# Up-projection weight sums formed by accumulating transfers instead of VectorE subtractions

## The chip, the cores and the metric

The kernel runs on one core of a Trainium2 chip. The metric is the device time of one execution in microseconds (us), the median of several runs. A core has a matrix engine (TensorE, PE in the profile; PEld is its weight load), VectorE (DVE), ScalarE (ACT), GpSimd (POOL) and SyncE (SP). Each engine works through its own queue in order. Transfers between DRAM and the on-chip memory (SBUF) are issued from the queues of SP, ACT or POOL and run on 16 transfer engines. Matrix products are summed in PSUM banks.

## What is computed

One decoder layer: two token mixers, a projection with a residual, a squared-ReLU MLP with a residual, and a gated embedding at the end. All inputs are float32. The change touches the first product of the MLP alone (cut from the reference; 512 tokens, `w_up` is 1024 x 4096, `w_down` 4096 x 1024):

```python
v = rms_norm(h, norm_pre_mlp[i])
ff = jnp.square(jax.nn.relu(v @ w_up[i])) @ w_down[i]
h = h + rms_norm(ff, norm_post_mlp[i])
```

## The kernel before

For precision every float32 operand is split into two parts, hi and lo (`split`, L59 to L61: ACT casts hi, DVE subtracts to get lo), and a product is three matmuls: hi by hi, hi by lo, lo by hi. A weight block is loaded into a `raw` tile of 128x1024 (512 KB), and `pair_of` splits it into a `whi`/`wlo` pair. There are six raw buffers and six pairs in this stage, two pools each, taken in turns.

The MLP works in four quarters. A quarter is two groups of the up product (`up_group`, L1020) and one down product (`down`, L1082), which runs 24 matmuls into each of eight accumulation sets (two column halves c by four token tiles t; each is copied or added into `facc` behind it). A scheduler that simulates the engines decides the order of each queue when the kernel is built, so the groups and the down product are interleaved in the queues.

A group multiplies 512 columns of `w_up` with all tokens, by a scheme with seven products of 2x2 blocks in place of eight. The weights of a group are four blocks of 512 rows by 256 columns: b11, b12, b21, b22 (first the row half, then the column half, as the kernel's names have it: `block(i, j)` is row half i, column half j, so `b21` is `block(1, 0)` and `b12` is `block(0, 1)`). The token side has the forms A11, A12, A22, S1 to S4, sums of blocks of the transposed activations, computed once in `to_forms` (L962). The weight sums of a group are made on DVE, in place in the raw tiles: L1048 (b12-b11, for S1), L1050 (t2 = b22 minus that, for S2), L1053 (b22-b12, for S3), L1063 (b21-t2, for A22). A product is 24 matmuls of 128x256 (`product`, L1004). X, Y and Z are PSUM banks; X is read in the middle of its accumulation by `side`, a copy on ACT; `finish` does the ReLU, the square and the split of the result for the down product.

A group is a generator in three steps. `steps` (L1071) lets step 1 of the next group (its A11 product) come between steps 2 and 3 of a group.

Of the kernel before, what the change touches and what calls it, by code (L numbers as in the profile page):

```python
# [11 lines left out]
AF = mybir.ActivationFunctionType  # L12
OP = mybir.AluOpType
# [15 lines left out]
def hybrid_layer(ctx: ExitStack, tc: tile.TileContext, x, p, w_in, w_branch_a, w_branch_b, w_out,  # L29
# [5 lines left out]
    x, p, out = x[0], p[0, 0], out[0]  # L35
# [12 lines left out]
    def k_rows(w, r0, nk, c0, n):  # L48
        return w[r0:r0 + nk * 128, c0:c0 + n].rearrange("(k p) c -> p k c", p=128)
# [47 lines left out]
    def raw_tile():  # L97
        i, pl = w_pool("raw")
        return pl.tile([128, 1024], FT, name="raw", tag="raw", bufs=RAWS[i])
# [787 lines left out]

    af = tc.alloc_tile_pool(name="af", reuse_waits="tile", bufs=1, side="right")
# [49 lines left out]
    with tc.tile_pool(name="wo", reuse_waits="tile", bufs=2, side="right") as wo:  # L938
# [23 lines left out]
        def to_forms(vn, t):  # L962
# [17 lines left out]
            dve.tensor_add(f1, f0, ps[1])  # L980
            into(A22, ps[1])
            dve.tensor_sub(f0, g0, f0)
            dve.tensor_sub(g0, f1, g0)
# [3 lines left out]
            dve.tensor_sub(g1, g1, g0)  # L987
# [25 lines left out]
    def finish(src, g, ch, th):  # L1013
        r = ff.tile([128, 2, 256], FT, name="r")
        act.activation(r, src, AF.Relu)
        act.activation(r, r, AF.Square)
        d = (slice(None), slice(2 * ch, 2 * ch + 2), slice(256 * th, 256 * th + 256))
        split(fbuf[g][0][d], fbuf[g][1][d], r)

    def up_group(g):  # L1020
        fbuf[g] = [ff.tile([128, 4, 512], FR, name=f"f{e}") for e in "hl"]

        def block(i, j):
            raw = raw_tile().rearrange("p (a b) -> p a b", a=4)
            sp.dma_start(raw, k_rows(w_up, i * 512, 4, g * 512 + j * 256, 256))
            return raw
# [10 lines left out]
        b11 = block(0, 0)  # L1037
        X = bank("up", 3)
        product(X, pair_of(b11, 4, 256), A11, True)
        m1 = side(X)  # L1040
        yield
        b21 = block(1, 0)
        Z = bank("tr", 2)
        product(Z, pair_of(b21, 4, 256), A12, True, True)
        dve.tensor_add(m1, m1, Z)
        finish(m1, g, 0, 0)
        b12, b22 = block(0, 1), block(1, 1)
        dve.tensor_sub(b11, b12, b11)  # L1048
        t2 = raw_tile().rearrange("p (a b) -> p a b", a=4)
        dve.tensor_sub(t2, b22, b11)  # L1050
        product(X, pair_of(t2, 4, 256), S2, False)
        u2 = side(X)
        dve.tensor_sub(b12, b22, b12)  # L1053
        Y = bank("up", 3)
        product(Y, pair_of(b12, 4, 256), S3, True)
        product(X, pair_of(b11, 4, 256), S1, False)
        w = side(X)
        dve.tensor_add(w, w, Y)
        finish(w, g, 1, 1)
        yield  # L1060
        product(X, pair_of(b22, 4, 256), S4, False, True)
        finish(X, g, 1, 0)
        dve.tensor_sub(b21, b21, t2)  # L1063
        product(Y, pair_of(b21, 4, 256), A22, False, True)
# [140 lines left out]
```

## Time and profile before

| | us |
|---|---|
| median of 3 runs | 1250.78 |
| lowest and highest | 1247.95 and 1251.27 |
| profiled execution, its time | 1249.47 |
| profiled execution, span of its instructions | 1247.7 |
| PE busy | 1199.2 (96%) |
| DVE busy | 794.2 (64%) |
| ACT busy | 629.9 (50%) |
| POOL busy | 169.4 (14%) |

The span is what the trace shows of the profiled execution; the rest of its time lies around it. Busy time of PE includes overlap of matmuls that follow each other, so a matmul of 283 ns of busy time takes less of the span than that. The MLP's products run from 843 us on.

### The profile page before, as it was taken

To read this page: it belongs to the slowest core of one execution; us is meant where nothing else is said; L and a number is where in the kernel's file an instruction comes from. 1 tells how busy PE (TensorE), PEld (TensorE's weight loads), DVE (VectorE), ACT (ScalarE), POOL (GpSimd) and SP (SyncE) were. 2 spreads that over 40 slices of the span, in tenths; PEclk is the share of its full clock that TensorE was granted. 3 is DMA by queue.
4 is the path that set the end of the run, shared out by engine and by line. 5 is a ranking of instruction groups with operands and counts; after the bars stand their busy time and mean duration, and the time that the engine had idled before them with its cause. 6 is when DMAs were issued, how large, how long until landed. Compare 5 with 4: busy or idle time off the path is not lost. (4 is left out here: it accounts for less than half of the span.)

```text
span 1247.7 us, 18829 instructions
## 1 busy us (share of the span) xinstructions
PE 1199.2 (96%) x7199; PEld 1031.9 (83%) x7199; DVE 794.2 (64%) x1448; ACT 629.9 (50%) x1273; POOL 169.4 (14%) x281
## 2 busy tenths in 40 slices
PE   7999999999999999999999999969999999999997
PEld 6888877777777889999978788859889899898885
DVE  6765687847877366867685455588447565474564
ACT  6555677757777334343443222367437346165242
POOL 2022332342321101111110111010000000000000
PEclk9999999999999999999999999989999999999999
DMA  6345221222112522222232984243324224136201
GB/s 180 104 113 158 61 65 43 52 55 56 51 43 68 152 85 69 68 68 68 72 80 86 279 218 123 97 152 118 102 69 150 83 74 151 51 119 203 85 18 67
DMA packets 129867, 123.43 MB, mean 99 GB/s; under 512 B 8385, under 2 KB 107633, under 8 KB 129778
## 3 DMA queue, kind: packets, MB, share of 16 engines
q1 hardware_dynamic: 119776, 105.39, 29.3%
q0 software_dynamic: 3200, 10.49, 2.9%
q10 hardware_dynamic: 6802, 6.36, 1.6%
q8 instruction: 56, 0.92, 0.3%
q14 instruction: 33, 0.27, 0.1%
HBM read 109.64 MB, written 12.58 MB: 98 GB/s over the span
## 5 line engine op out<-in xcount | busy, mean ns | idle before, releaser
L60 ACT CAST whi<-raw 128x1024 fp32r<-128x1024 f32 (+1 forms) x199 | 207.7, 1046 | 216.3 <-PE acc L1094 61.7
L61 DVE TENSOR_TENSOR wlo<-raw,whi 128x1024 fp32r<-128x1024 f32 (+1 forms) x181 | 220.9, 1224 | 140.1 <-ACT whi L60 139.6
L133 PE MATMUL ps<-whi,uh 128*128 128x256 f32 (+1 forms) x512 | 147.9, 290 | 1.5 <-DVE kcd L257 0.5
L135 PE MATMUL ps<-whi,ul 128*128 128x256 f32 (+1 forms) x512 | 146.6, 286 | 0.0
L134 PE MATMUL ps<-wlo,uh 128*128 128x256 f32 (+1 forms) x512 | 146.2, 286 | 0.2 <-DVE wlo L61 0.2
L82 PE MATMUL ps<-uh,whi 128*128 128x512 f32 x288 | 118.2, 410 | 0.0
L84 PE MATMUL ps<-uh,wlo 128*128 128x512 f32 x288 | 114.7, 398 | 0.3 <-DVE wlo L61 0.3
L83 PE MATMUL ps<-ul,whi 128*128 128x512 f32 x288 | 114.7, 398 | 0.0
L1093 PE MATMUL acc<-wlo,fh 128*128 128x512 f32 x256 | 100.9, 395 | 0.0
L1092 PE MATMUL acc<-whi,fh 128*128 128x512 f32 x256 | 100.7, 395 | 0.0
L1094 PE MATMUL acc<-whi,fl 128*128 128x512 f32 x256 | 100.0, 394 | 0.0
L133 PEld LDWEIGHTS ps<-whi,uh 128*128 128x128 f32 x512 | 96.6, 189 | 4.0 <-PE cps L84 0.7
L134 PEld LDWEIGHTS ps<-wlo,uh 128*128 128x128 f32 x512 | 96.9, 189 | 1.3 <-DVE wlo L61 0.5
L135 PEld LDWEIGHTS ps<-whi,ul 128*128 128x128 f32 x512 | 96.8, 189 | 0.6 <-issue 0.2
L469 ACT ACTIVATE P<-ps_s,nm 128x128 f32<-128x128 f32 (+3 forms) x128 | 67.7, 530 | 28.6 <-DVE nm L467 26.1
L467 DVE TENSOR_REDUCE nm<-ps_s 128x1 f32<-128x128 f32 (+3 forms) x128 | 61.2, 484 | 25.9 <-PE ps_s L465 25.0
L61 DVE TENSOR_TENSOR ptl<-tr,pth 128x512 fp32r<-128x512 f32 x82 | 55.5, 683 | 23.4 <-ACT pth L60 23.1
L84 PEld LDWEIGHTS ps<-uh,wlo 128*128 128x128 f32 x288 | 54.1, 188 | 12.6 <-DVE wlo L61 0.4
L83 PEld LDWEIGHTS ps<-ul,whi 128*128 128x128 f32 x288 | 54.2, 188 | 10.2
L82 PEld LDWEIGHTS ps<-uh,whi 128*128 128x128 f32 x288 | 54.2, 188 | 10.0
L1092 PEld LDWEIGHTS acc<-whi,fh 128*128 128x128 f32 x256 | 48.1, 188 | 11.3
L1093 PEld LDWEIGHTS acc<-wlo,fh 128*128 128x128 f32 x256 | 48.3, 189 | 11.0
(349 smaller groups left out, 2958.4 us busy)
## 6 DMA issues: line engine op xcount, KB each, us to landing
raw<-in_w_in_dram SPq DMA_DIRECT2D x58, 512.0 KB, 3.8
raw<-in_w_up_dram SPq DMA_DIRECT2D x32, 512.0 KB, 3.7
raw<-in_w_down_dram SPq DMA_DIRECT2D x32, 512.0 KB, 4.4
raw<-in_w_in_dram SPq DMA_DIRECT2D x17, 256.0 KB, 3.5
raw<-in_w_branch_a_dram SPq DMA_DIRECT2D x8, 512.0 KB, 8.1
raw<-in_w_branch_b_dram SPq DMA_DIRECT2D x32, 128.0 KB, 5.9
raw<-in_w_out_dram SPq DMA_DIRECT2D x8, 512.0 KB, 4.3
raw<-in_w_ple_gate_dram SPq DMA_DIRECT2D x8, 512.0 KB, 4.8
```

The lines of the kernel that those rows point to most:

```text
L60: act.copy(hi, src)
L61: (lo_eng or dve).tensor_sub(lo, src, hi)
L82: rec.append(pe.matmul(ps, lh, rh, start=first, stop=False).ins)
L83: pe.matmul(ps, lh, rl, start=False, stop=False)
L84: pe.matmul(ps, ll, rh, start=False, stop=last)
L133: rec.append(pe.matmul(o, stat[0][:, k, s], hi[:, i], start=(k == 0), stop=False).ins)
L134: pe.matmul(o, stat[0][:, k, s], lo[:, i], start=False, stop=False)
L135: pe.matmul(o, stat[1][:, k, s], hi[:, i], start=False, stop=(k == NK - 1))
L469: act.activation(pt[:, :nk], ps[:, :nk], AF.Exp, bias=nm, accum_out=sums[:, h:h + 1])
L1092: pe.matmul(ps, fh[:, k % 4, s], hi[:, k % 2], start=(k == 0), stop=False)
L1093: pe.matmul(ps, fh[:, k % 4, s], lo[:, k % 2], start=False, stop=False)
L1094: pe.matmul(ps, fl[:, k % 4, s], hi[:, k % 2], start=False, stop=(k == NK - 1))
```

## The change

A block sum is now made by a transfer: `block(i, j, to)` issues from POOL a load of the block with `accum_op=OP.add`, which adds the block to what the raw tile `to` holds. The tile q1 holds b11 and later b11+b12. The tile q2 holds b22, then b22+b12, then b22+b12+b11, then b22+b12+b11+b21, and each of the four states is split into a pair of its own. So that blocks are only added, some forms of the token side change their sign (in `to_forms`), and `finish` takes a sign for the two results that come out negative. Per group there are three plain loads (before: four), four accumulating ones, and no subtraction of blocks on DVE; three raw tiles are used instead of five. The split of b22 comes ahead of those of the sums.

```diff
--- before.py
+++ after.py
@@ -977,14 +978,14 @@
             g0, g1 = (facc[:, t - 2, g * 512:g * 512 + 512].rearrange("p (k t) -> p k t", k=4)
                       for g in range(2))
             act.copy(f0, ps[0])
-            dve.tensor_add(f1, f0, ps[1])
+            dve.tensor_sub(f1, ps[1], f0)
             into(A22, ps[1])
             dve.tensor_sub(f0, g0, f0)
-            dve.tensor_sub(g0, f1, g0)
+            dve.scalar_tensor_tensor(g0, f1, -1.0, g0, op0=OP.mult, op1=OP.subtract)
             into(S2, g0)
             into(S3, f0)
             into(S1, f1)
-            dve.tensor_sub(g1, g1, g0)
+            dve.scalar_tensor_tensor(g1, g1, -1.0, g0, op0=OP.mult, op1=OP.subtract)
             into(S4, g1)
         proj_n(w_out, (mgh, mgl), NK, evac_o)
     mg.release()
@@ -1010,9 +1011,9 @@
                     pe.matmul(ps[:, c], l[:, k, cs], r[:, k], start=f and n == 0,
                               stop=e and n == 2, skip_group_check=True)
 
-    def finish(src, g, ch, th):
+    def finish(src, g, ch, th, sign=1.0):
         r = ff.tile([128, 2, 256], FT, name="r")
-        act.activation(r, src, AF.Relu)
+        act.activation(r, src, AF.Relu, scale=sign)
         act.activation(r, r, AF.Square)
         d = (slice(None), slice(2 * ch, 2 * ch + 2), slice(256 * th, 256 * th + 256))
         split(fbuf[g][0][d], fbuf[g][1][d], r)
@@ -1020,9 +1021,13 @@
     def up_group(g):
         fbuf[g] = [ff.tile([128, 4, 512], FR, name=f"f{e}") for e in "hl"]
 
-        def block(i, j):
+        def block(i, j, to=None):
+            src = k_rows(w_up, i * 512, 4, g * 512 + j * 256, 256)
+            if to is not None:
+                pool.dma_start(to, src, accum_op=OP.add)
+                return to
             raw = raw_tile().rearrange("p (a b) -> p a b", a=4)
-            sp.dma_start(raw, k_rows(w_up, i * 512, 4, g * 512 + j * 256, 256))
+            sp.dma_start(raw, src)
             return raw
 
         def bank(tag, bufs):
@@ -1034,34 +1039,32 @@
             act.copy(d, src)
             return d
 
-        b11 = block(0, 0)
+        def halved(raw):
+            return pair_of(raw, 4, 256)
+
+        q1 = block(0, 0)
         X = bank("up", 3)
-        product(X, pair_of(b11, 4, 256), A11, True)
+        product(X, halved(q1), A11, True)
         m1 = side(X)
         yield
-        b21 = block(1, 0)
         Z = bank("tr", 2)
-        product(Z, pair_of(b21, 4, 256), A12, True, True)
+        product(Z, halved(block(1, 0)), A12, True, True)
         dve.tensor_add(m1, m1, Z)
         finish(m1, g, 0, 0)
-        b12, b22 = block(0, 1), block(1, 1)
-        dve.tensor_sub(b11, b12, b11)
-        t2 = raw_tile().rearrange("p (a b) -> p a b", a=4)
-        dve.tensor_sub(t2, b22, b11)
-        product(X, pair_of(t2, 4, 256), S2, False)
+        q2 = block(1, 1)
+        b22 = halved(q2)
+        Y = bank("up", 3)
+        product(Y, halved(block(0, 1, q2)), S3, True)
+        product(X, halved(block(0, 0, q2)), S2, False)
         u2 = side(X)
-        dve.tensor_sub(b12, b22, b12)
-        Y = bank("up", 3)
-        product(Y, pair_of(b12, 4, 256), S3, True)
-        product(X, pair_of(b11, 4, 256), S1, False)
+        product(X, halved(block(0, 1, q1)), S1, False)
         w = side(X)
         dve.tensor_add(w, w, Y)
-        finish(w, g, 1, 1)
+        finish(w, g, 1, 1, -1.0)
         yield
-        product(X, pair_of(b22, 4, 256), S4, False, True)
-        finish(X, g, 1, 0)
-        dve.tensor_sub(b21, b21, t2)
-        product(Y, pair_of(b21, 4, 256), A22, False, True)
+        product(X, b22, S4, False, True)
+        finish(X, g, 1, 0, -1.0)
+        product(Y, halved(block(1, 0, q2)), A22, False, True)
         dve.tensor_add(u2, u2, Y)
         finish(u2, g, 0, 1)
         yield
```

The scheduler orders the queues anew. Three places follow; in tile names, the number tells one tile from another.

POOL's queue, from the loads of the post-norm weights to the end. `xt` are the residual inputs of the token tiles, `rsr` the power operations of the norms:

```order
-L950 DMA xt<-in_x_dram 128x1024 x2
-L930 TENSOR_TENSOR rsr<-rsb,half 128x1 x3
...
+L951 DMA xt<-in_x_dram 128x1024 x2
+L1027 DMA raw<-in_w_up_dram 128x4x256
+L931 TENSOR_TENSOR rsr<-rsb,half 128x1 x2
...
+L1027 DMA raw<-in_w_up_dram 128x4x256
+L931 TENSOR_TENSOR rsr<-rsb,half 128x1 x2
+L1027 DMA raw<-in_w_up_dram 128x4x256
+L931 TENSOR_TENSOR rsr<-rsb,half 128x1
+L896 DMA w_post_9133<-in_norm_post_mlp_dram 128x1024
+L1027 DMA raw<-in_w_up_dram 128x4x256 x29
```

Three of the 32 accumulating transfers now stand among the power operations of `w_out`'s evacuation, the other 29 stand by themselves, with nothing of another kind between them.

ACT's queue at the end of the first down product, groups 2 and 3, before (`raw_9953` and `raw_9958` are sums, `raw_9955` is b22 and `raw_9916` the sum for A22 of group 2, `raw_10159` b21 of group 3; `facc` rows are the copies behind accumulation sets 7 and 8):

```order
L1103 COPY facc_8003<-acc_9864 128x512
L60 CAST whi_9992<-raw_9953 128x1024
L60 CAST whi_10020<-raw_9559 128x1024
L60 CAST whi_10061<-raw_10058 128x1024
L1103 COPY facc_8003<-acc_9890 128x512
L60 CAST whi_10091<-raw_9955 128x1024
L60 CAST whi_10125<-raw_9916 128x1024
L60 CAST whi_10162<-raw_10159 128x1024
```

The same place now. `raw_9947` is q2 of group 2, cast for S3, for S2 and for A22; `raw_9557` is its q1, for S1; `raw_10053`, `raw_10151` and `raw_10187` are group 3's q1, b21 (for A12) and q2 (as b22):

```order
L1106 COPY facc_8003<-acc_9858 128x512
L60 CAST whi_9955<-raw_9947 128x1024
L60 CAST whi_10015<-raw_9557 128x1024
L1106 COPY facc_8003<-acc_9884 128x512
L60 CAST whi_9984<-raw_9947 128x1024
L60 CAST whi_10056<-raw_10053 128x1024
...
L60 CAST whi_10116<-raw_9947 128x1024
L60 CAST whi_10153<-raw_10151 128x1024
L60 CAST whi_10189<-raw_10187 128x1024
```

Three casts of one tile stand in the queue with other casts between them, where three different tiles stood; the casts of group 3's b21 and b22 stand behind the last of them.

PE's queue in group 3 now, where S3's product ends (`up_10193` is its bank, `up_10055` is X, `up_10295` is X of group 4):

```order
L1011 MATMUL up_10193<-s3h_8641,whi_10195 128x256
L1011 MATMUL up_10193<-s3l_8642,whi_10195 128x256
L1011 MATMUL up_10193<-s3h_8641,wlo_10196 128x256
L1011 MATMUL up_10055<-s2h_8639,whi_10224 128x256
L1011 MATMUL up_10055<-s2l_8640,whi_10224 128x256
L1011 MATMUL up_10295<-a11h_8631,whi_10296 128x256
L1011 MATMUL up_10295<-a11l_8632,whi_10296 128x256
L1011 MATMUL up_10055<-s2h_8639,wlo_10225 128x256
```

S2 follows S3 directly; before, S2 stood ahead of S3 there, and both weights came from separate tiles.

## Rows read from the trace of the kernel before

**Rows 1.** Busy tenths of the span in 40 slices, and granted clock, from the page.

```profile
PE   7999999999999999999999999969999999999997
...
PEclk9999999999999999999999999989999999999999
```

**Rows 2.** Windows: stretch, length, busy us (instructions) by engine, clock, transfer share, GB/s.

```profile
880.00:964.00 84.00, 84.00 (x530) 75.44 (x529) 44.82 (x46) 44.32 (x61) 0.00 (x0) 1.00 0.33 101
964.00:1048.00 84.00, 84.00 (x530) 75.41 (x529) 49.50 (x54) 39.60 (x54) 0.00 (x0) 1.00 0.33 101
```

**Rows 3.** Who waited for whom, 843 to 1117: total us, times, longest.

```profile
ACT whi L60 <- PE acc L1094: 59.7, 20, 16.4
...
PEld tr L1010 <- DVE a22l L61: 0.5, 1, 0.5
```

**Rows 4.** The chain that ended last, in order of time: start, us, what.

```profile
843.50 4.74 PE tr L1010 x24
...
862.17 16.80 PE up L1010 x144
...
929.22 2.87 PE tr L1010 x24
932.09 11.20 PE up L1010 x96
```

**Rows 5.** ACT in order of time: start, us, line, idle before and its releaser.

```profile
847.09 0.62 ACT L60 CAST s4h<-facc 128x512 fp32r<-128x512 f32 x1 [1.18 <-DVE facc L987]
...
918.09 0.59 ACT L1103 COPY facc<-acc 128x512 f32<-128x512 f32 x1 [5.00 <-PE acc L1094]
923.68 0.59 ACT L1103 COPY facc<-acc 128x512 f32<-128x512 f32 x1 [5.00 <-PE acc L1094]
925.08 1.05 ACT L60 CAST whi<-raw 128x1024 fp32r<-128x1024 f32 x1 [0.82 <-PE acc L1094]
```

**Rows 6.** Groups by line from 760 us on: busy us, mean ns, idle before.

```profile
L61 DVE TENSOR_TENSOR wlo<-raw,whi 128x1024 fp32r<-128x1024 f32 x104 | 126.5, 1222 | 84.7 <-ACT whi L60 84.4
...
L1063 DVE TENSOR_TENSOR raw<-raw 128x1024 f32<-128x1024 f32 x8 | 9.8, 1220 | 0.1
...
L936 DVE SCALAR_TENSOR_TENSOR xt<-facc,rsr,xt 128x512 f32<-128x512 f32 x8 | 5.6, 747 | 1.7 <-POOL rsr L930 1.7
...
L982 DVE TENSOR_TENSOR facc<-facc 128x512 f32<-128x512 f32 x2 | 1.4, 686 | 0.0
...
L60 ACT CAST whi<-raw 128x1024 fp32r<-128x1024 f32 x72 | 75.4, 1050 | 109.0 <-PE acc L1094 59.7 <-PE up L1010 40.7 <-PE tr L1010 4.3
```

**Rows 7.** Transfers in 843 to 848 (two rows) and in 929 to 934 (last).

```profile
q1 hardware_dynamic: 528, 0.52, 36.2%
...
raw<-in_w_up_dram SPq DMA_DIRECT2D x1, 512.0 KB, 3.6
...
raw<-in_w_up_dram SPq DMA_DIRECT2D x1, 512.0 KB, 4.5
```

**Rows 8.** Transfer issues of the whole span: KB each, median us to landing.

```profile
xt<-in_x_dram POOLq DMA_DIRECT2D x4, 512.0 KB, 5.3
```

**Rows 9.** Transfer issues as instructions: POOL's groups (busy, mean ns), SyncE's (min/median/max ns).

```profile
L503 POOL DMA_DIRECT2D yl_d<-yl x16 | 10.7, 668 | 3.5 <-POOL yl L501 3.2 <-PE tr L158 0.3
...
L950 POOL DMA_DIRECT2D xt<-in_x_dram x4 | 2.2, 551 | 4.4 <-ACT sqs L922 3.6 <-DVE vn L958 0.8
...
L1025 SPq DMA_DIRECT2D raw<-in_w_up_dram x25: 367/368/368, 843.5 to 1096.5; - x25
```

**Rows 10.** Windows of PE: stretch, length, busy us, clock, transfer share, GB/s.

```profile
839.00:842.00 3.00, 0.22 (x2) 0.50 0.00 0
...
845.00:848.00 3.00, 3.00 (x19) 0.64 0.49 157
848.00:851.00 3.00, 3.00 (x28) 1.00 0.00 0
```

**Rows 11.** DVE in order of time, 804 to 806.

```profile
804.02 1.22 DVE L1063 TENSOR_TENSOR raw<-raw 128x1024 f32<-128x1024 f32 x1
805.15 0.68 DVE L946 TENSOR_TENSOR facc<-acc,w_post 128x512 f32<-128x512 f32 x1
```

## The prediction

> **What bounds the kernel now.** I read the page's table of busy tenths first: TensorE (PE) stands at 9 nearly everywhere, at full clock, and the last big dip is slice 27, where the MLP begins [rows 1]. Then the windows table: in the up and down products PE is busy 84.00 of 84.00 us in each stretch of 84, which is one quarter of the MLP (two groups of up blocks and one down product) [rows 2]. Then who waits for whom there: PE's only own entry is 0.5 us; ScalarE (ACT) and VectorE (DVE) wait for PE [rows 3]. So from 843 us to the MLP's end no work on DVE is on the path. Taking DVE work away there gains nothing, and any wait that PE gets is added in full: there is no slack behind it.
>
> **What is removed.** Four subtractions of 128x1024 per group, 32 in all, at 1.22 us [rows 6]: 39 us of DVE time. 28 of them (groups 1 to 7) lie under full PE: worth 0. The four of group 0 run before 843 or just after; one of them holds up the evacuation at 805.15 by about a microsecond [rows 11], and the path goes on from there through a transfer and DVE work that stay. I take 0 there and keep 1 us of gain as the bound. One of the four plain loads per group also leaves SyncE's queue (32 become 24); those loads were hidden: 0.
>
> **What is added, cheap parts.** In the S forms two subtractions per token tile become three-operand ones, four in all; by the nearest rows 0.75 instead of 0.69 us [rows 6], 0.2 us in sum. The sign in the ReLU is a scale of an instruction that is there already: 0. GpSimd (POOL) issues 32 transfers; it has nothing else in this stage, so the issue time itself hides, but in the first group a transfer stands ahead of three power operations on which the start at 843 depends: at 0.9 us an issue, between 0 and 3 us; I take 0, since its block's split lies before DVE's next residual anyway.
>
> **What is added, the part that counts.** Four accumulating transfers per group. Three of them write the same tile, q2, one after the other: +b12 (weights for S3), +b11 (for S2), +b21 (for A22). Each must wait until the split of the sum before it has been read by both ACT and DVE, and each next split waits until the transfer has landed. Before, the three sums were 1.22 us of DVE each from blocks loaded long ahead. Now they are a serial chain, per link one split (cast 1.05 us, subtraction 1.22 us, 2.3 together [rows 6]) and one accumulate, which I call x: from the end of the subtraction to the sum being there.
>
> *The size of x.* No accumulating transfer is in this trace. Nearest row: a plain load of the same 512 KB block with the same 1 KB rows, alone in its window, lands 3.6 us after issue, and its packets keep the 16 engines busy for 36.2% of 5 us, 1.8 us [rows 7]. So 1.8 us is transfer and 1.8 us the rest. POOL's issue grows from 551 ns at 128 rows of a transfer to 668 at 256 [rows 9], about 0.9 at 512, against 0.37 on SyncE [rows 9]: +0.5. A sum must read its destination as well; I count the transfer twice: 1.8+3.6+0.5 = 5.9 alone. Beside another load the same load takes 4.5 instead of 3.6 [rows 7]; half of that 0.9, and 0.1 to 0.2 of hand-offs, make **x = 6.5**. Bounds: 4.1 (as the plain load, 3.6+0.5) and 10.6 (twice the 5.3 us of POOL's 512 KB loads [rows 8]).
>
> *Where the chain meets PE.* I follow groups 2 and 3 in ACT's new order (the fence of ACT rows). T is the end of the seventh of the eight accumulation sets of the down product, 923.7 in the trace of before; the next pair of weight buffers comes free 1.4 us later, and the first split of before starts there [rows 5]. b22 is split and b12 added earlier, in the 14 us before T. Then: S3's split ends at T+3.7; b11 lands T+3.7+x; S2's split ends T+6.0+x; b21 lands T+6.0+2x. ACT's queue is in order: behind A22's cast stand those of A12 and of the next group's b22. One cast and three subtractions are 4.7 us, so next b22's split ends T+10.7+2x. Then the next group's chain: b12 lands T+10.7+3x, its split ends T+13.0+3x, b11 lands T+13.0+4x, the split of S2 ends T+15.3+4x.
>
> PE needs that last pair after the eighth accumulation set (5.6 us: the copies that follow one set each are 5.59 apart [rows 5]) and nine products of 24 matmuls at 2.8 us (11.20 for 96 [rows 4]): T+30.8, and has four matmuls, 0.5 us, that do not need its low half. PE is late by 4x+15.3-31.3 = **4x-16**. At x = 6.5 that is 10 us; about 4 of them show at the A12 product of the second group, whose cast stands behind A22's, and 6 at S2. A22 of the second group has another 18 us ahead of it and does not bind. Three quarters (groups 2/3, 4/5, 6/7) have this order: 30 us. The chain starts from PE's place in each quarter, so a late quarter doesn't start the next one earlier.
>
> Groups 0 and 1: group 1's b22 is split behind the S forms, whose last cast is at 847.09 [rows 5], A22's cast, three finish steps and its own: about 853.2. S2's cast is ready at 853.2+2x+3.4; PE reaches it 48 matmuls into the piece that starts at 862.17 [rows 4], 867.8. Late by 2x-11.2: 1.8 us.
>
> *Clock.* After idle stretches at the start of the MLP the granted clock was 0.50 and came back to 1.00 only by 848 [rows 10]; the first product ran at 4.74 us instead of 2.87 [rows 4], 1.9 us more. While PE waits for the chain a low clock costs nothing; after the last wait of each quarter I add 1.9 once: 5.7.
>
> Sum: 0.2+30+1.8+5.7 = 37.7 us. The profiled execution took 1249.47, of which 1247.7 are span, so 1287.2 there; the median of the three runs is 1.3 above it. I predict **1289 us**.
>
> **Rivals.**
> *The accumulate is cheap.* If x is at most 4.1, as the plain load, 4x-16 is 0.4, groups 0 and 1 have slack, and nothing waits: 1250 to 1253. For it: the transfer is 1.8 of 3.6 us, and a second read might overlap the first. Against: it would have to cost nothing. The Trainium skill (DMA: Bandwidth & Descriptors, Anatomy of one DMA — SWDGE (gpsimd) path) gives a GpSimd-issued transfer about 2.0 us plus its bytes at 436 GB/s; with the bytes counted twice that is an estimate of 4.4 us, by which the sum would be some 5 us, 1256; the plain rows here, 3.6 and 5.3, are above its 3.2 for one pass.
>
> *The accumulate is dear.* If reading, adding and writing back follow each other row by row, x is 9 or more: 3x20, 6.8 at groups 0 and 1, 5.7 clock, and 1 to 2 at the start, where DVE's split of S3 stands ahead of the residual of the last token tile: 1324. At 10.6: 3x26.4+10+6+3, 1348. For it: the POOL loads of 512 KB with four times longer rows already took 5.3. The Trainium skill (Collectives: The Full Stack, The bandwidth ceiling: the fold count and why AG ≠ RS ≠ AR) holds that an add in flight costs its second source read and no cycles of its own, a measured factor of 1.93; that speaks against this rival, and no run here shows it yet.
>
> *Faster.* Mechanism: the four subtractions of group 0 all stand on the DVE path into 843 and x is under 4, so that no chain binds. Price: up to 4x1.22 = 4.9 us off, 1246. It decides from x = 4.0 down. Against: between 835 and 847 there is no such subtraction on DVE in before, so at most one or two count.
>
> **How the numbers follow.** A measurement of this kernel tells 0.3%, 3.75 us, from no change. Forecast (x 5 to 8, 1264 to 1313): 0.50. Dear (1313 to 1350): 0.22. Cheap or nearly so: 0.23, of which 0.13 within 0.3% and 0.10 slower (1255 to 1264). Faster: 0.05. So slower 0.82, same 0.13, faster 0.05. The range from 1252 to 1338 leaves out about 0.10 below and 0.08 above.
>
> **What would show it.** In the trace of after: accumulating transfers from issue to landing near 6 to 7 us; PE no longer at 84 of 84 in a quarter but with two waits in each, at A12 and S2 of the odd group, put down to the casts of these pairs, the casts in turn to the transfers; ACT idle before its casts for the transfer and no longer for PE; a dip in the granted clock in each quarter; DVE some 39 us less busy. I would be wrong by the size of x, entering twelvefold; by the buffers (if b22's longer stay holds back A12's pair, PE waits where I have none); or if the first group's transfers delay the S forms, so that PE starts later than 843 us.

## The result, and the profile after

The changed kernel takes 1308.53 us (median; 1306.51 to 1313.89) against 1251.03 for the kernel before: a ratio of 1.0472, 95% interval 1.0445 to 1.0499. The profiled execution took 1309.35, of which 1307.4 are span, so 59.7 us of span were added to the 1247.7 of before. The forecast was 1289, its range 1252 to 1338.

Where they were added is read best at one product that begins each quarter of the MLP, A12 of the first group of a pair (24 matmuls `tr<-a12`). Between these starts PE has the same products to do in both kernels. In the rows of PE in order of time of the changed kernel:

```profile
850.17 0.58 PE L1011 MATMUL tr<-a12h,whi 128*128 128x256 f32 x1
...
941.82 0.28 PE L1011 MATMUL tr<-a12h,whi 128*128 128x256 f32 x1
...
1039.86 0.28 PE L1011 MATMUL tr<-a12h,whi 128*128 128x256 f32 x1
...
1138.32 0.28 PE L1011 MATMUL tr<-a12h,whi 128*128 128x256 f32 x1
```

The first line is the start of the MLP, which was 843.50 [rows 4]. The same starts in every kernel of this study give the table on which the experiments are read (us; the last stretch runs from the fourth start to the end of the span, and the time is the median). Two shifts of work have to be kept in mind: in e2 and e5, 17 matmuls (2.0 us) of the first quarter already stand ahead of its start, and in e7 the second, third and fourth starts have the S3 product of their own pair (24 matmuls, 2.8 us) ahead of them, so its first quarter holds 2.8 us more work than elsewhere and its last stretch 2.8 less:

| kernel | start | 1st quarter | 2nd | 3rd | last stretch | time |
|---|---|---|---|---|---|---|
| before | 843.50 | 85.56 | 83.84 | 83.84 | 150.96 | 1251.03 |
| **after** | 850.17 | 91.65 | 98.04 | 98.46 | 169.08 | 1308.53 |
| added in after | 6.7 | 6.1 | 14.2 | 14.6 | 18.1 | 57.5 |
| e1_dve_adds | 844.87 | 86.26 | 84.03 | 85.67 | 151.67 | 1257.16 |
| e2_dead_transfers | 879.07 | 82.42 | 83.84 | 83.83 | 150.94 | 1283.09 |
| e9_plain | 843.13 | 85.03 | 88.54 | 87.35 | 157.65 | 1264.76 |
| e5_twice | 863.88 | 114.10 | 131.24 | 129.81 | 193.97 | 1436.22 |
| e8_a22_dve | 849.72 | 90.71 | 93.09 | 93.41 | 158.17 | 1287.24 |
| e11_last_a22 | 847.16 | 91.04 | 97.67 | 98.38 | 164.15 | 1304.34 |
| e6_late_groups | 846.82 | 86.13 | 98.13 | 98.33 | 168.89 | 1299.73 |
| e7_early | 842.97 | 95.30 | 98.72 | 98.80 | 165.71 | 1302.40 |
| e3_only_s1 | 844.65 | 86.91 | 86.29 | 92.61 | 154.44 | 1267.07 |
| e10_only_s3 | 848.44 | 87.33 | 84.33 | 85.66 | 157.14 | 1262.30 |

The page's busy tenths of the changed kernel, the answer to [rows 1]: one dip in each of the quarters after the first and two in the last stretch, where there was one at the MLP's start alone; the granted clock is below 9 tenths in the same slices.

```profile
PE   7999999999999999999999999499979979978997
...
PEclk9999999999999999999999999789989989988999
```

Windows of the changed kernel (stretch, length, busy us and instructions of PE, PEld, DVE, ACT and POOL, clock, transfer share, GB/s). PE no longer fills its stretches, as it did in [rows 2], and the two shortest ones are at the lowest clock, 0.87:

```profile
880.00:964.00 84.00, 79.13 (x451) 69.54 (x450) 28.48 (x29) 35.46 (x49) 7.75 (x6) 0.95 0.54 123
964.00:990.00 26.00, 22.24 (x164) 21.61 (x164) 13.73 (x15) 15.76 (x23) 3.85 (x3) 0.87 0.61 112
990.00:1048.00 58.00, 57.55 (x302) 48.71 (x301) 22.89 (x26) 19.10 (x25) 3.40 (x3) 1.00 0.41 109
1048.00:1100.00 52.00, 44.97 (x304) 42.69 (x304) 22.10 (x24) 26.09 (x38) 6.93 (x6) 0.87 0.66 142
```

Who waited for whom from 843 to 1200 (total us, times, longest). In [rows 3] ACT's casts waited for PE; now they wait as long for the transfers, and PE waits for the casts and for a copy that stands behind them:

```profile
ACT whi L60 <- DMA raw<-in_w_up_dram: 66.0, 17, 5.8
ACT whi L60 <- PE acc L1097: 61.2, 17, 17.2
...
PE up L1011 <- ACT whi L60: 13.7, 9, 3.6
PE tr L1011 <- ACT whi L60: 9.1, 3, 3.2
PE up L1011 <- ACT side L1039: 7.2, 5, 3.6
```

The chain in groups 2 and 3 can be followed link by link. POOL's transfers of that quarter, in order of time: each waits for a split's second half (`wlo`) on DVE.

```profile
940.41 1.28 POOL L1027 DMA_DIRECT2D raw<-in_w_up_dram  x1 [16.42 <-DVE wlo L61]
948.99 2.59 POOL L1027 DMA_DIRECT2D raw<-in_w_up_dram  x2 [7.30 <-DVE wlo L61]
959.90 1.28 POOL L1027 DMA_DIRECT2D raw<-in_w_up_dram  x1 [8.31 <-DVE wlo L61]
969.07 1.28 POOL L1027 DMA_DIRECT2D raw<-in_w_up_dram  x1 [7.89 <-DVE wlo L61]
```

And the casts on ACT that wait for them:

```profile
946.39 2.00 ACT L60 CAST whi<-raw 128x1024 fp32r<-128x1024 f32 x2 [3.79 <-DMA raw<-in_w_up_dram]
...
955.03 2.94 ACT L60 CAST whi<-raw 128x1024 fp32r<-128x1024 f32 x3 [4.80 <-DMA raw<-in_w_up_dram]
957.88 0.58 ACT L1039 COPY side<-up 128x512 f32<-128x512 f32 x1
...
966.47 1.05 ACT L60 CAST whi<-raw 128x1024 fp32r<-128x1024 f32 x1 [0.82 <-DMA raw<-in_w_up_dram]
...
977.16 1.99 ACT L60 CAST whi<-raw 128x1024 fp32r<-128x1024 f32 x2 [5.84 <-DMA raw<-in_w_up_dram]
```

The pairs are: 940.41 to 946.39 (+b11, S2), 948.99 to 955.03 (+b21, A22; the casts of A12 and of the next b22 follow it in the same row), 959.90 to 966.47 (next group, +b12, S3), 969.07 to 977.16 (next group, +b11, S2). The four links are 6.0, 6.0, 6.6 and 8.1 us, 6.7 in the mean, and between them lie the splits. (The second transfer in the row of 948.99 is that of S1 in the next group; it is not of this chain.) PE waits at the ends of the second and the fourth:

```profile
957.08 0.58 PE L1011 MATMUL tr<-a12h,whi 128*128 128x256 f32 x1 [2.88 <-ACT whi L60]
...
958.50 0.58 PE L1011 MATMUL up<-s1h,whi 128*128 128x256 f32 x1 [0.64 <-ACT side L1039]
...
978.26 0.58 PE L1011 MATMUL up<-s2h,whi 128*128 128x256 f32 x1 [3.60 <-ACT whi L60]
```

In the rows of PE a matmul of this shape takes 0.28 us at a granted clock of 1.00; here the first after each wait takes 0.58 and those behind it 0.41. The granted clock is 0.50 (1.2 of 2.4 GHz) from 957 to 962 and again from 978 to 983, both times after PE had stood idle for about 3 us (2.88 and 3.60).

### The profile page after: what moved, and what is told of

It reads as the page before. It is cut to its first block, busy times and chain, and to the rows that moved or that the text cites. A ratio compares the mean times of both kernels' runs of the same rounds, so it can differ in the third digit from the quotient of the medians.

```text
span 1307.4 us, 18865 instructions
## 1 busy us (share of the span) xinstructions
PE 1221.4 (93%) x7199; PEld 1049.7 (80%) x7199; DVE 760.2 (58%) x1416; ACT 629.2 (48%) x1273; POOL 211.3 (16%) x313
## 3 DMA queue, kind: packets, MB, share of 16 engines
q0 software_dynamic: 20096, 27.27, 11.5%
## 5 line engine op out<-in xcount | busy, mean ns | idle before, releaser
L1027 POOL DMA_DIRECT2D raw<-in_w_up_dram x32 | 41.3, 1316 | 328.5 <-DVE wlo L61 251.3
L61 DVE TENSOR_TENSOR ptl<-tr,pth 128x512 fp32r<-128x512 f32 x82 | 55.6, 683 | 23.7 <-ACT pth L60 23.4
L1095 PEld LDWEIGHTS acc<-whi,fh 128*128 128x128 f32 x256 | 47.8, 188 | 12.4 <-ACT whi L60 1.1
```

What stands on the lines that cost most here:

```text
L61: (lo_eng or dve).tensor_sub(lo, src, hi)
L1095: pe.matmul(ps, fh[:, k % 4, s], hi[:, k % 2], start=(k == 0), stop=False)
```

## The experiments

The theory under test is the prediction's: PE is late in a quarter because four accumulating transfers and the splits between them stand in series (late by 4x-16), and not because of the new order of products, of the added traffic, or of a fixed price of each transfer.

### The order without the transfers

e1_dve_adds keeps the changed order and signs and forms the sums by DVE additions from blocks that are loaded plainly.

```diff
+        def plus(to, b):
+            dve.tensor_add(to, to, b)
+            return to
...
-        product(Z, halved(block(1, 0)), A12, True, True)
+        b21 = block(1, 0)
+        product(Z, halved(b21), A12, True, True)
...
-        q2 = block(1, 1)
+        q2, b12 = block(1, 1), block(0, 1)
...
-        product(Y, halved(block(0, 1, q2)), S3, True)
-        product(X, halved(block(0, 0, q2)), S2, False)
+        product(Y, halved(plus(q2, b12)), S3, True)
+        product(X, halved(plus(q2, q1)), S2, False)
...
-        product(X, halved(block(0, 1, q1)), S1, False)
+        product(X, halved(plus(q1, b12)), S1, False)
...
-        product(Y, halved(block(1, 0, q2)), A22, False, True)
+        product(Y, halved(plus(q2, b21)), A22, False, True)
```

> The changed kernel's signs, products and order of splits (S3 first, b22 ahead of the sums, the sums in place in q1 and q2), but each sum is a DVE addition of 1.22 us from a block that SyncE has loaded. No accumulating transfer is left. Theory 'chain' (PE waits for the links of split and accumulate on one tile): a link is now 1.2 us instead of 6.4 or more, 4x-16 is negative, so the time of the kernel before, 1247 to 1255 us. Rival 'order' (the loss comes from the new order of products and from in-place tiles that are held longer): most of the 57 us stays, 1290 to 1308.

Measured: 1257.16 us, 1.0055 (1.0037 to 1.0074). The order and signs cost 5 to 7 us by themselves (4.8 of span in the profiled execution, in parts of 0.2 to 1.8 over start and stretches; 6.9 by the ratio); the other 50 or so come with the transfers. The theory's upper end was missed by 2 us: the prediction had put the order at 0.2.

### The traffic without the chain

e2_dead_transfers is the kernel before, with four accumulating transfers per group into a spare tile that nothing reads.

```diff
+    spare = af.tile([128, 4, 256], FT, name="spare")
+    pool.memset(spare, 0.0)
...
+        def dead(i, j):
+            pool.dma_start(spare, k_rows(w_up, i * 512, 4, g * 512 + j * 256, 256), accum_op=OP.add)
...
+        dead(0, 1)
+        dead(0, 0)
+        dead(0, 1)
...
+        dead(1, 0)
```

> The kernel before, and in each group four accumulating transfers of the same blocks from GpSimd into a spare tile that nothing reads: the changed kernel's issue work and more than its traffic (32 such transfers on top of 32 plain loads), without a wait of any compute engine for them. Theory 'chain': 1250 to 1258, a few us at most where weight loads land later. Rival 'traffic' (transfers and GpSimd's issues slow the rest): near the changed kernel, 1285 to 1310.

Measured: 1283.09 us, 1.0265 (1.0243 to 1.0286). By the total alone this would speak for the traffic. The windows say otherwise; PE is full in the same stretches as in [rows 2], at a transfer share of 0.78 and 0.62:

```profile
880.00:964.00 84.00, 84.00 (x527) 75.46 (x526) 43.24 (x44) 43.76 (x60) 14.10 (x11) 1.00 0.78 168
964.00:1048.00 84.00, 84.00 (x532) 75.46 (x531) 49.96 (x53) 39.14 (x52) 7.69 (x6) 1.00 0.62 146
```

All of the loss lies before the MLP, 35.6 us at its start. There PE waits for the norm (waits of PE, 780 to 1200), and POOL in order of time shows why:

```profile
PE tr L158 <- DVE vn L958: 29.4, 3, 15.8
```

```profile
837.09 1.31 POOL L1032 DMA_DIRECT2D spare<-in_w_up_dram  x1 [2.30 <-DMA spare<-in_w_up_dram]
837.88 1.62 POOL L930 TENSOR_TENSOR rsr<-rsb,half 128x1 f32<-128x1 f32 x2
...
853.10 1.28 POOL L1032 DMA_DIRECT2D spare<-in_w_up_dram  x1 [7.61 <-DMA spare<-in_w_up_dram]
853.88 1.61 POOL L930 TENSOR_TENSOR rsr<-rsb,half 128x1 f32<-128x1 f32 x2
```

Each transfer waits at the head of POOL's queue until the one before has landed on the same tile, and the norm's power operations (L930) stand behind it. By POOL's rows the 32 transfers are issued from 780.18 to 1012.76: 15 before the MLP's first start, 11 in the first quarter, 6 in the second and none in the third. The first quarter, which holds three more of them than a quarter of the changed kernel, takes 82.42 us (some 84.4 with the 2.0 us of its work that stand ahead of the start), the second 83.84. So the traffic and the issues of such transfers cost a quarter nothing here, while a transfer that waits on POOL costs much where POOL has other work. The traffic rival falls; the one kernel shows both.

### The size of x: a plain transfer, and two in a row

e9_plain takes the addition out of the transfer; e5_twice issues each transfer a second time.

```diff
-                pool.dma_start(to, src, accum_op=OP.add)
+                pool.dma_start(to, src)
```

> The changed kernel with the accumulation left out of the 32 transfers from GpSimd: each is a plain load over the tile, with the same waits (so the weight sums are not formed). What a transfer takes beyond a plain one falls away: x from 6.4 to about 4.5 to 5 (3.6 of the plain load, the longer issue, hand-offs). Theory 'chain' with 12 links in the three later quarters: 12 times 1.4 to 1.9, and 3 to 5 us at the start and in the first quarter, so 1280 to 1289. Rival 'order': 1305 to 1310. Were the price of the accumulation itself all there is: 1250 to 1255.

```diff
                 pool.dma_start(to, src, accum_op=OP.add)
+                pool.dma_start(to, src, accum_op=OP.add)
```

> Each accumulating transfer is issued twice in a row on the same tile, so its block is added twice and the output is wrong by that; all else is as in the changed kernel. Measured so far: one accumulating transfer lands 6.4 us (median) after issue, the changed kernel takes 1308.5 us. Theory (a serial chain, x in the prediction's words): if the second waits for the first, x doubles to about 12.8; a quarter is late by 4x minus a constant, so each of the three later quarters and the last one loses 4 x 6.4 = 26 us more, groups 0 and 1 lose 2 x 6.4 = 13 us more, the start 5 to 10 more: 1400 to 1430 us, with quarters of about 124 us instead of 98. Rival (each transfer has a fixed price, as from contention or queue time, 58/32 = 1.8 us): 32 more of them cost 58 us, spread evenly: about 1366, quarters of about 112. Rival (the two overlap on the queue, x grows by the issue alone, 1.3 us): quarters grow by 5 us, 1330.

Measured: e9_plain 1264.76 (1.0118; 1.0088 to 1.0147), below the 1280 to 1289 that were expected of it. From issue to landing its transfers take 4.2 us (median) instead of 6.4, and the mean link of the second quarter is 4.75 us instead of 6.7: that is the fall of 1.4 to 1.9 that was reckoned with. What was not reckoned with is the rest. PE's longest wait in those two quarters is 1.2 us, and the granted clock is 1.00 in the second and the third quarter where the changed kernel has 0.93, so the time at the lower clock is gone too. The start and the first quarter fell by 13.7 us together where 3 to 5 were expected, and the last stretch by 11.4 where its four links make 6 to 8.

e5_twice took 1436.22 (1.1495; 1.1471 to 1.1518), a little above the chain theory's 1400 to 1430 and far above the fixed price's 1366; its quarters, 131 and 130, are longer than the 124 that were expected. In its second quarter POOL and ACT show a link of two transfers:

```profile
1026.73 1.28 POOL L1027 DMA_DIRECT2D raw<-in_w_up_dram  x1 [7.40 <-DVE wlo L61]
1035.64 1.28 POOL L1028 DMA_DIRECT2D raw<-in_w_up_dram  x1 [7.63 <-DMA raw<-in_w_up_dram]
```

```profile
1041.60 1.99 ACT L60 CAST whi<-raw 128x1024 fp32r<-128x1024 f32 x2 [12.35 <-DMA raw<-in_w_up_dram]
```

From 1026.73 to 1041.60 are 14.9 us; the four links of the quarter are 12.4, 15.0, 13.8 and 14.9, mean 14.0. With these two kernels the law can be held against rows. PE's lateness is the time from the quarter's A12 to the second group's S2, less nine products of 2.80 us, 25.2:

| kernel, 2nd quarter | A12 | S2 of the odd group | late | mean link x | 4x-16 |
|---|---|---|---|---|---|
| e9_plain | 928.16 | 956.92 | 3.6 | 4.75 | 3.0 |
| after | 941.82 | 978.26 | 11.2 | 6.7 | 10.7 |
| e5_twice | 977.98 | 1042.70 | 39.5 | 14.0 | 40.1 |

Over a range of three in x the lateness follows 4x-16 within 0.6 us. The third quarters agree as well (late 2.4, 11.3 and 37.3, against 1.8, 10.7 and 37.8). So the theory's main term is shown: these four links and the splits between them are what PE is late by. (Links and lateness are read from the same trace; the table tests the number of links and the constant, not the size of x.)

### One link taken out

e8_a22_dve forms A22's sum on DVE, in all groups; e11_last_a22 does so in the last group alone.

```diff
-        product(Z, halved(block(1, 0)), A12, True, True)
+        b21 = block(1, 0)
+        product(Z, halved(b21), A12, True, True)
...
-        product(Y, halved(block(1, 0, q2)), A22, False, True)
+        dve.tensor_add(q2, q2, b21)
+        product(Y, halved(q2), A22, False, True)
```

> As the changed kernel, but the block b21, which is loaded for the A12 product anyway, is kept and added to q2 by one DVE addition instead of the third accumulating transfer on q2. One of the four links between two odd-group S2 pairs becomes a 1.2 us addition, so the chain theory has a quarter late by 3x - 14.8 instead of 4x - 16: 5.2 us less in each of the three later quarters (98 to 93), about 5 less in the first quarter (91.6 to about 87) and about 5 less at the end, the start unchanged at 850: 1281 to 1290 us. Fixed price of 1.8 us for each transfer: 8 fewer, 1294, and no quarter by more than 4 us shorter. If the wait sits only at S2 and S3, not at A22 and what stands behind it on ACT: 1305 or more.

```diff
+        if g == 7:
+            dve.tensor_add(q2, q2, b21)
+        else:
+            block(1, 0, q2)
+        product(Y, halved(q2), A22, False, True)
```

> The changed kernel with a single transfer taken out: the last group's A22 block is added by DVE from the plain block, 31 accumulating transfers stay. In the changed kernel the last stretch lost 18.1 us where the quarters lost 14; there the cast of this pair waits for its transfer at the head of ACT's queue with the side copy of S1's sum behind it, and PE waits for that copy. Theory (this one link at the head of ACT's queue is on the path to the end): start and the three quarters as in the changed kernel, the last stretch 158 to 161 us instead of 169, 1298 to 1301 us. Rival (it is worth what it is worth in a quarter, 5 us): 1303.5. Rival (it is behind the last wait, since S2's transfer is what binds): no change, 1306 to 1310.

Measured: e8_a22_dve 1287.24 (1.0305; 1.0290 to 1.0321): the second and third quarters fall by 5.0 us each, as 3x-14.8 wants it, the last stretch by 10.9 where 5 were expected, the first quarter by 0.9 instead of 5, the start hardly; the total is as expected because the misses cancel. e11_last_a22 1304.34 (1.0436; 1.0415 to 1.0457): the last stretch falls by 4.9, not by the 8 to 11 that I expected; that is the size of the first rival. So the last stretch is a quarter like the others, late by its chain, plus about 5 us from this one cast. The two runs agree: e8, which also takes out the link of the pair's first group, gained 10.9 there, about the 5.0 of a quarter and these 4.9. In the changed kernel ACT and PE show it there:

```profile
1183.05 1.99 ACT L60 CAST whi<-raw 128x1024 fp32r<-128x1024 f32 x2 [3.41 <-DMA raw<-in_w_up_dram]
1184.95 0.58 ACT L1039 COPY side<-up 128x512 f32<-128x512 f32 x1
```

```profile
1185.58 0.58 PE L1011 MATMUL up<-s1h,whi 128*128 128x256 f32 x1 [3.62 <-ACT side L1039]
```

The cast of A22's pair waits for its transfer, the copy of S2's sums stands behind it on ACT, and S1's product, which writes the same bank, waits for the copy. In e11_last_a22 that wait of PE is 0.57 us:

```profile
1178.82 0.39 PE L1011 MATMUL up<-s1h,whi 128*128 128x256 f32 x1 [0.57 <-ACT side L1039]
```

The start in this kernel is 847.16 against 850.17, although nothing before the last group is changed: about 3 us of difference at the start can lie between two executions of the same work, and I read no start more finely than that.

### The first two groups without transfers

e6_late_groups takes e1's additions for groups 0 and 1 and the transfers for groups 2 to 7.

```diff
-    groups = [up_group(g) for g in range(8)]
+    groups = [(up_group_dve if g < 2 else up_group)(g) for g in range(8)]
```

> The changed kernel with groups 0 and 1 formed by DVE additions; groups 2 to 7 by accumulating transfers as they were. In the changed kernel's trace the MLP's A12 product of group 0 starts 6.7 us later than before and the first quarter is 6.1 us longer. Theory 'chain': these 12.8 us go and the three later quarters stay, 1294 to 1298. If the late start came from other things than the transfers in front of the forms: 1301 to 1303.

Measured: 1299.73 (1.0398; 1.0369 to 1.0426), 1.7 us above what was expected. The first quarter loses 0.6 instead of 6.1 and the start 3.3 instead of 6.7; the later quarters keep their 98.13 and 98.33. The quarters' losses are their own, and don't come from the start.

### The next group's head moved up

e7_early puts the load of q2, b22's split and S3's transfer and split one step earlier in the program, meant to stand on ACT ahead of the A22 cast of the group before.

```diff
         yield
...
+        q2 = block(1, 1)
+        b22 = halved(q2)
+        s3 = halved(block(0, 1, q2))
...
-        q2 = block(1, 1)
-        b22 = halved(q2)
...
-        product(Y, halved(block(0, 1, q2)), S3, True)
+        product(Y, s3, S3, True)
```

> The same transfers as in the changed kernel, but the load of q2, the split of b22, the transfer of b12 and the split of S3's sum of a group are put ahead of the group's S2 by one step of the table, so that on ACT and DVE they stand ahead of the A22 cast of the group before instead of behind it; the chains of two neighbouring groups then run beside each other on two tiles. Chain theory: between the two S2 pairs of a quarter stand three transfers' waits instead of four, with one or two more splits: a quarter late by about 3x - 13.7, or 2x - 5.3 at A22, 5.5 to 7.5 plus 2 of clock instead of the 14 measured: quarters of 91 to 94 us, 1285 to 1298 us in all. Rival (the price is by the transfer, or from what the transfers do to the loads beside them): nothing changes, 1305 to 1312. Rival (the earlier b12 transfer stands ahead of b21's in POOL's queue and delays it): longer than 1312.

Measured: 1302.40 (1.0420; 1.0402 to 1.0437). The quarters did not shorten (98.72 and 98.80): my expectation of 91 to 94 was wrong. The chain was relieved at the place that I had looked at (PE waits 0.17 us for S2 of the odd group, at 964.18, instead of 3.60), and other waits came in its stead. One thing that the expectation had left as it was is x. The page of this run has its transfers 2.0 us slower than those of the changed kernel (6.4):

```profile
raw<-in_w_up_dram POOLq DMA_DIRECT2D x32, 512.0 KB, 8.4
```

So every wait for a transfer is longer here than was reckoned; why they land later in this order is not shown. Up to S2 of the odd group PE is late by 6.2 us (964.18 less 938.27, less seven products of 2.80 us and two matmuls), within the 5.5 to 7.5 that were expected; but it gets there by waits behind a cast, and further ones follow. ACT in order of time, and PE:

```profile
946.35 1.05 ACT L60 CAST whi<-raw 128x1024 fp32r<-128x1024 f32 x1 [6.09 <-DMA raw<-in_w_up_dram]
...
949.14 0.58 ACT L1039 COPY side<-up 128x512 f32<-128x512 f32 x1
```

```profile
949.77 0.58 PE L1011 MATMUL up<-s1h,whi 128*128 128x256 f32 x1 [2.89 <-ACT side L1039]
```

The cast that waits 6.09 us is A22's, by its place in ACT's order; the copy for which PE waits is four instructions behind it. The next weight cast on ACT waits 2.24 us for another transfer (951.96), so by the same reading not all the casts came to stand ahead of A22's, as was meant. It is the pattern of the last stretch, now in every quarter; at 978.60 PE waits another 3.86 us for such a copy. What did fall is the start, to 842.97: with the casts of group 0's transfers placed earlier, nothing is lost there. With the 2.8 us of shifted work counted where they belong, the first quarter is 92.5 and the last stretch 168.5, as long as in the changed kernel within 0.9, so the start is all that this order gained. This run doesn't tell the chain from a price by the transfer, and where the rest of its 14.9 us per quarter comes from (PE's waits from 936 to 1037 sum to 9.0, the remainder is time at the lower clock by the lengths of the products) I read from the rows alone.

### Transfers off the chain

e3_only_s1 and e10_only_s3 keep one accumulating transfer per group and form the other sums as e1 does.

The diffs are against e1_dve_adds.

```diff
-        product(X, halved(plus(q1, b12)), S1, False)
+        product(X, halved(block(0, 1, q1)), S1, False)
```

> The changed kernel's order and signs, the three sums on q2 by DVE additions (b12 and b21 loaded plainly and kept), and only S1's block (q1 + b12) by an accumulating transfer: 8 of 32 are left, and they are on no chain, since q1 is read once, early, and the sum is wanted some 20 us later. Chain theory: as with all sums on DVE, 1254 to 1262 us, quarters of 84 to 86 us. Fixed price of 1.8 us for each transfer: 1257 + 14 = 1271, quarters 3.6 us longer than with all sums on DVE. If an accumulating transfer disturbs the down loads beside it, the same 3 us or more per quarter.

```diff
-        product(Y, halved(plus(q2, b12)), S3, True)
+        product(Y, halved(block(0, 1, q2)), S3, True)
```

> The changed kernel's order and signs, with one accumulating transfer per group, that of S3 (q2 + b12), and the other three sums by DVE additions from blocks loaded plainly. The transfer waits only for b22's split and holds up only S3's cast: one link of the chain per group instead of four per pair of groups in series. (In the run with S1's transfer alone I had overlooked that it had to wait for the DVE addition that reads q1; its cast then stood 7 us waiting at the head of ACT's queue, with the next A11 cast behind it.) Chain theory: a lone link is late by x + 18.9 - 31.3, below zero, so nothing is lost but what the order costs: 1255 to 1263 us; if the S3 cast still holds the casts behind it, up to 1270, and the trace shows ACT waiting for the transfer at that cast. Fixed price of 1.8 us per transfer: 1257 + 14 = 1271, spread evenly over the quarters.

Measured: e3_only_s1 1267.07 (1.0142; 1.0125 to 1.0159), above my 1254 to 1262. The transfer is not free here: it writes q1, and must wait until DVE has read q1 for S2's sum. POOL and ACT in the third quarter:

```profile
1017.94 1.28 POOL L1027 DMA_DIRECT2D raw<-in_w_up_dram  x1 [68.13 <-DVE raw L1046]
```

```profile
1025.54 1.99 ACT L60 CAST whi<-raw 128x1024 fp32r<-128x1024 f32 x2 [6.98 <-DMA raw<-in_w_up_dram]
```

ACT's cast of S1 waits 6.98 us, the next A11's cast stands behind it, and PE waits 4.0 us for that; this quarter lost 6.9 us against e1's, the other two 0.6 and 2.3. e10_only_s3 took 1262.30 (1.0099; 1.0080 to 1.0117), within what was expected: its second and third quarters (84.33 and 85.66) are e1's (84.03 and 85.67). In the second one ACT does wait for such a transfer:

```profile
951.06 1.05 ACT L60 CAST whi<-raw 128x1024 fp32r<-128x1024 f32 x1 [5.08 <-DMA raw<-in_w_up_dram]
```

but PE has no wait from there to the quarter's end. A transfer for which PE doesn't wait, neither for its sum nor for what stands behind it, costs such a quarter nothing, and a fixed price of 1.8 us each, two in a quarter, is excluded there. What it lies above e1 (10.4 us of span in the two profiled executions, 5 in the medians) is at the start (3.6), in the first quarter (1.1) and in the last stretch (5.5), where a cast that waits 5.55 us for a down load (ACT, 1143.57) stands ahead of a side copy for which PE waits 4.09 us (1145.16). Whether the transfers beside that load made it late is not shown.

None of these versions is faster than the kernel before: even with all sums on DVE the new order takes 0.5% longer.

## Why the prediction was right, step by step

The total lies in the range and the mechanism is the one forecast, but the total is not where the sum put it: the forecast added 37.7 us of span, and 59.7 were added. The range was made that wide for the size of x, but x came out within 0.2 of what was taken, and the 22 us come from other terms. By the forecast's own sum, 59.7 us would need an x of about 8. That the time still lies in the range is in part luck.

- **Removed work is worth nothing.** Right. DVE is busy 760.2 us instead of 794.2 (34 less, 39 was forecast). No run takes this work out by itself, but in no stretch did time come back.
- **The chain.** Right in mechanism and place: PE waits at the A12 product behind A22's cast and at S2 of the odd group. The forecast put the issue of the next group's b12 at T+10.7+2x, T+23.7 with x at 6.5; it stands at 959.90, T+23.6 (T, the end of the seventh set, is 936.3; the copy that follows it starts at 936.41). e9, the changed kernel and e5 lie on 4x-16.
- **The size of x.** 6.5 was taken; from issue to landing the median of 32 is 6.4 us, and the links are 6.7 in the mean of that quarter. The parts of the estimate came out differently: the issue costs 1.28 us, not 0.9. The cheap rival fell with x above 4.1, the dear one with x below 9.
- **A quarter** lost 14.2 and 14.6 against 11.9. Its terms: late 11.2 against 10 (0.7 by x, the rest by the splits and hand-offs), and clock after the last wait 2.8 against 1.9: the 26 matmuls of S2 and the start of A11 take 5.82 us, 978.26 to 984.08, where 26 at full clock take 3.0. The clock between the two waits cost nothing of its own, as was argued: the lateness at the second wait is the chain's, with or without it.
- **Groups 0 and 1** lost 6.1 against 1.8. PE waits there 2.56 us for S2, near the forecast, and 0.92 for a down block's cast; of the remaining 2.6, 2.1 are the lower clock after the wait (granted 0.79 from 874 to 882; 26 matmuls take 5.09 us, 876.98 to 882.07, where 3.0 is full clock), which I had added in three quarters and forgotten in this one. The last 0.5 stay open.
- **The last stretch** lost 18.1; it was counted as a quarter. The step that failed is "A22 of the second group has another 18 us ahead of it and does not bind": its product doesn't, but its cast stands on ACT ahead of a copy that PE wants much earlier. e11_last_a22 gives this link back 4.9 us.
- **The start** was taken as 0, with bounds of 0 to 3; it lost 6.7 here and 3.7 in e11_last_a22, whose work up to there is the same. This is the step that failed outright. I had looked at POOL's issue time in front of the power operations, which is hidden, and held that the first group's splits lie ahead of DVE's next residual. They do stand ahead of it, but wait for the transfers. ACT at the start of the MLP of the changed kernel:

```profile
830.20 1.99 ACT L60 CAST whi<-raw 128x1024 fp32r<-128x1024 f32 x2 [3.67 <-DMA raw<-in_w_up_dram]
...
842.48 1.99 ACT L60 CAST whi<-raw 128x1024 fp32r<-128x1024 f32 x2 [5.63 <-DMA raw<-in_w_up_dram]
...
845.41 0.57 ACT L980 COPY facc<-tr 128x512 f32<-128x512 f32 x1
```

  Behind the second of them stand the S forms' casts and a copy for which PE waits 5.0 us. With the casts placed earlier the loss is gone (e7_early, 842.97). With the transfers it is 3.7 to 6.7 (e11, e8 and the changed kernel), without them 1.4 to 3.3 (e1, e6): these ranges all but touch, so how many of the 6.7 us are the transfers' is known to a few us only.
- **The order itself** was put at 0.2 and is worth 5 to 7 us by e1; in e1 it lies mostly at the start and in the third quarter. How much of it is in each of the items above, no run shows.

Sum of the misses: start 6.5, first quarter 4.3, second and third 5.0, last 6.2, together 22.0 over the forecast's 37.7, which is the 59.7 of the span. Forecast and outcome have the same main cause, the waits for the transfers. About half of what was short stands behind a waiting cast on ACT's queue: the start (6.5, of which some 3 can lie between executions) and the copy in the last stretch (4.9). The rest is time at the lower clock (2.1 in the first quarter, and 0.9 and 1.3 more than forecast in the second and the third), a slightly larger x, the cast of the down block, and what stays open, the order among it.

## What to carry to other kernels

In this kernel an addition that moved from an engine into a transfer was paid in latency, not in engine time: if several sums are written to one tile in turn, count each as the time from issue to landing, in series with the readers between them, and multiply by the number of links between two deadlines. Take that time from a trace of the same order of work, since it can move with the order (6.4 us here, 8.4 in e7_early). Then look at what stands behind each waiting instruction on its engine's queue, copies for other consumers above all; in each later quarter PE's first long wait was for a cast behind a waiting one (957.08), not for the product that reads the sum. The transfers for which PE did not wait cost the quarters of e10_only_s3 nothing. And before the trade is made, ask whether the engine that it relieves is on the path at all.

## What the runs showed of the hardware

Transfer issues on the page of the changed kernel (KB each, median us from issue to landing), the group of POOL's issue instructions (busy, mean ns), and its queue (packets, MB, share of 16 engines):

```profile
raw<-in_w_up_dram POOLq DMA_DIRECT2D x32, 512.0 KB, 6.4
raw<-in_w_down_dram SPq DMA_DIRECT2D x32, 512.0 KB, 5.5
raw<-in_w_up_dram SPq DMA_DIRECT2D x24, 512.0 KB, 4.3
```

```profile
L1027 POOL DMA_DIRECT2D raw<-in_w_up_dram x32 | 41.3, 1316 | 328.5 <-DVE wlo L61 251.3
...
q0 software_dynamic: 20096, 27.27, 11.5%
```

And the same of e9_plain, whose source differs by the addition alone:

```profile
raw<-in_w_up_dram POOLq DMA_DIRECT2D x32, 512.0 KB, 4.2
```

```profile
L1027 POOL DMA_DIRECT2D raw<-in_w_up_dram x32 | 24.1, 753 | 300.4 <-DVE wlo L61 219.7
...
q0 software_dynamic: 7808, 27.27, 7.1%
```

The kernel before has 3200 packets and 2.9% on this queue from its other work. So a 512 KB block in rows of 1 KB is 528 packets with the addition and 144 without, POOL issues it in 1.3 us instead of 0.75, and it lands in 6.4 instead of 4.2. Its packets keep the 16 engines busy for 3.6 us instead of 1.7 ((11.5% of 1307.4 - 2.9% of 1247.7)/32, and likewise for 7.1% of 1261.7). The Trainium skill (Collectives: The Full Stack, The bandwidth ceiling: the fold count and why AG ≠ RS ≠ AR) has an addition in flight cost its second source read, a measured factor of 1.93 between AllGather and ReduceScatter; the packets' time here, a factor of 2.1, agrees. With the Trainium skill's fit for the SWDGE path (DMA: Bandwidth & Descriptors, Anatomy of one DMA — SWDGE (gpsimd) path), 2.0 us plus the bytes at 436 GB/s, the runs don't agree: it gives estimates of 3.2 us for the plain transfer and, with the bytes counted twice, of 4.4 for the accumulating one, and 4.2 and 6.4 were measured.

The down loads beside the transfers land in 5.5 us instead of 4.4 (5.4 in e2_dead_transfers, where PE stays full): slower, but hidden there, and in the changed kernel but for one wait of PE of 0.92 us for a down block's cast, in the first quarter.
